# A hybrid decoder layer on one core: sample rows in four transfers beside x's parts, and the delta rule's state loads spread over its first steps

## The chip, the cores and the metric

The kernel runs on one core of a Trainium2 chip. Its time is the device time of one execution in microseconds (us); the lower the better. TensorE does the matrix products, VectorE and ScalarE the elementwise work, GpSimd small copies, memsets and some transfers, and SyncE (SP) issues most transfers.

## The reference, cut to what matters

One layer of a decoder trunk runs over 256 prompt tokens and over 8 sequences of 4 sample tokens, which go through the same weights:

```
proj = x @ w_in                                    # 2048 -> 11280 columns, split in 11 parts
y_a  = (gB * conv3(gC * h)) @ w_a_out              # short convolution mixer
q, k, v = silu(conv4([q | k | v]))                 # width-4 causal convolution
o, S = gated_delta_rule(l2norm(q), l2norm(k), v, g, beta, S0)   # 8 heads of 128, chunks of 64
y_b  = (rmsnorm(o) * silu(z)) @ w_b_out
merged = sigmoid(m_a) * y_a + sigmoid(m_b) * y_b
x = LN(ALPHA * x + merged @ w_o)
x = LN(ALPHA * x + relu(x @ w_up)**2 @ w_down)     # 2048 -> 8192 -> 2048
```

The prompt starts from zero states; the samples bring convolution states and a 128 x 128 state S0 for each head and sequence. All data are float32.

## The kernel before, in words

**The stream of weight blocks.** All products are one stream of blocks, numbered i. A block is 512 rows by 256 columns of a weight matrix, 512 KB, loaded by SP (`load`, L169). For precision each weight is split in two: ScalarE rounds it (`split_hi`, L177) and VectorE takes the rest (`split_lo`, through the helper `tt`, L140). The activations x are split likewise into `xh` and `xl`, with the 2048 features on 16 groups of 128 partitions and 288 columns (256 prompt, 32 sample tokens). `matmuls(i)` issues 24 matrix products for a block: for each of 4 groups of rows and 2 halves of columns the three products of L202, L203 and L204 (xh with hi, xl with hi, xh with lo). A list `fill` gives functions that are called one after each three products, so that other TensorE work stands between them. The first eight blocks belong to two column groups in turn, so that blocks 0 and 1 need features 0 to 511 only, blocks 2 and 3 the next, and so on.

**The order of the work.** It is written out by hand. In iteration i the program issues the high split of block i + 3, one step of a generator `sgen` (the delta rule's side work), one step of its helper `aux`, the low split of block i + 3, the work on finished sums (`due`), and then the products of block i. Engines take their instructions in this order, each its own; a waiting instruction holds up all that follow on its engine. High and low parts have four buffers each, so the split of block i + 3 waits for the products of block i - 1.

**The start.** x comes in four parts of 512 features (`xr0` to `xr3`), `xr0` in two halves, one issued by ScalarE (L728) and one by SP (L731). The sample tokens come in one transfer (L729) as 128 rows: quarter j of the features of token t is row 32 j + t, so that one row holds 512 features. TensorE turns blocks of 128 x 128 (transposes, L771 for the prompt, L757 for the samples); ScalarE casts the result to `xh` (L775, L760), VectorE takes `xl`. Eleven small products on a cleared tile (`warm_up`, L718) stand before, and four more between the samples' transposes and block 0. All of the samples' features are turned at once, after the prompt's first part; the prompt's other three parts are turned in the fills of blocks 1, 3 and 5. On GpSimd a one-element copy (L742) waits for the third part `xr2`; behind it stand 19 small loads of convolution states, convolution weights and norm weights (L745 to L751), which `hist_tiles` turns on TensorE before block 6 (L791 to L796).

**The delta rule.** Finished q, k and v columns go through `conv_evac`: a memset and a copy of the state on GpSimd (L261, L262), copies and a product on ScalarE (L263, L264, L266), three products on VectorE (L143), then SiLU on ScalarE (L276, L281), one block later. `sgen` first runs `gates` (from block 10, one step for each block), and then `gdn(G)` for the two halves of four heads, the first from block 20 on at the earliest. In `gdn`, four loads on GpSimd bring the states S0 (512 KB each, L911), three memsets clear `kqm`, `U128` and `aT` (L929, L931), and the first two steps turn k and q (L943) and take squares and copies (L945, L947); in the third step the sample's keys are spread by ScalarE into `wide` (L961), and in the fourth TensorE turns that (L965). `warm_up`, `x_sample` and `x_steps` are used only at the start.

## Time and profile before

| | before |
|---|---|
| median of 3 runs | 1711.37 us (1710.66 to 1711.64) |
| the profiled execution | 1709.66 us, of which its span 1707.8 |
| mean granted TensorE clock | 0.992 |
| TensorE busy | 1684.7 us (99%) |
| VectorE, ScalarE, GpSimd busy | 1012.4, 727.0, 123.5 us |
| read from memory | 270.19 MB, 163 GB/s over the span |

Busy times are shares of the whole span. With TensorE at 99%, the time can shrink only where TensorE waits or runs at a lower clock. The span counts from the first to the last instruction; some 1.9 us lie around it. A timeline row of the profile gives start, duration, engine, line, operation, output and inputs, how many, and in brackets how long the engine was idle before and what ended that. PE is TensorE, DVE VectorE, ACT ScalarE, POOL GpSimd.

### The profile page before, as it was taken

How to read it: one execution, taken by the hardware profiler on the slowest of the kernel's cores; microseconds unless marked ns; L12 is line 12 of the kernel's file. 1: busy time of each engine (PE TensorE's matmuls, PEld its weight loads, DVE VectorE, ACT ScalarE, POOL GpSimd, SP SyncE). 2: the span in 40 equal slices, each digit the busy share in tenths (PEclk: the TensorE clock that was granted, in tenths of full speed). 3: DMA queues.
4: the chain of work that ended last, by engine and by line, in shares of the span. 5: the costliest groups of instructions: out<-in, count | busy, mean ns of one | idle time of the engine just before them, and what ended most of it. 6: DMA issues, size and time to landing. Idle time of an engine off the chain costs nothing.

```text
span 1707.8 us, 31019 instructions
## 1 busy us (share of the span) xinstructions
PE 1684.7 (99%) x13040; PEld 1667.2 (98%) x13040; DVE 1012.4 (59%) x1292; ACT 727.0 (43%) x1045; POOL 123.5 (7%) x223
## 2 busy tenths in 40 slices
PE   8989999999999999999999999999999999999997
PEld 7989999999999999999999999999999999999996
DVE  4568795748544444456778844565445654466575
ACT  4675536433643334334445533344334433344331
POOL 2122331013300000000010000000000000000000
PEclk9999999999999999999999999999999999999998
DMA  8454356444655555555575555555555555555552
GB/s 242 149 173 150 112 172 208 146 135 137 186 177 164 170 161 169 164 165 165 158 198 176 169 166 165 167 163 166 168 161 160 171 163 170 163 162 160 173 160 69
DMA packets 272537, 279.69 MB, mean 164 GB/s; under 512 B 12109, under 2 KB 267533, under 8 KB 272265
## 3 DMA queue, kind: packets, MB, share of 16 engines
q1 hardware_dynamic: 267066, 265.26, 49.9%
q0 software_dynamic: 4352, 11.67, 2.5%
q8 instruction: 102, 1.67, 0.4%
q10 hardware_dynamic: 980, 0.79, 0.2%
q14 instruction: 37, 0.30, 0.0%
HBM read 270.19 MB, written 7.48 MB: 163 GB/s over the span
## 4 chain that ended last, share of the span: by engine, by line
PE 90%; DVE 2%; ACT 1%; issue 1%; POOL 0%; ACTq 0%; DVEq 0%
PE acc L202 29%; PE acc L203 29%; PE acc L204 29%; PE g L1069 1%; DVE lo L140 1%; DVE w L143 1%; PE g L1057 0%; PE g L1236 0%; PE g L1239 0%; PE g L1188 0%; PE g L1216 0%; PE g L598 0%; PE g L657 0%; DVE v L143 0%; ACT hi L177 0%
## 5 line engine op out<-in xcount | busy, mean ns | idle before, releaser
L140 DVE TENSOR_TENSOR lo<-raw,hi 128x1024 fp32r<-128x1024 f32 (+1 forms) x500 | 613.2, 1230 | 541.6 <-ACT hi L177 539.4
L177 ACT CAST hi<-raw 128x1024 fp32r<-128x1024 f32 (+1 forms) x500 | 518.1, 1039 | 756.5 <-PE acc L203 701.6
L202 PE MATMUL acc<-xh,hi 128*128 128x288 f32 x1408 | 421.4, 299 | 0.0
L204 PE MATMUL acc<-xh,lo 128*128 128x288 f32 x1408 | 416.4, 296 | 0.0
L203 PE MATMUL acc<-xl,hi 128*128 128x288 f32 x1408 | 416.4, 296 | 0.0
L202 PE MATMUL acc<-dh,hi 128*128 128x290 f32 x1024 | 303.9, 297 | 0.0
L203 PE MATMUL acc<-dl,hi 128*128 128x290 f32 x1024 | 303.3, 296 | 0.0
L204 PE MATMUL acc<-dh,lo 128*128 128x290 f32 x1024 | 302.7, 296 | 0.0
L204 PE MATMUL acc<-hh,lo 128*128 128x288 f32 x1024 | 302.3, 295 | 0.0
L203 PE MATMUL acc<-hl,hi 128*128 128x288 f32 x1024 | 302.3, 295 | 0.0
L202 PE MATMUL acc<-hh,hi 128*128 128x288 f32 x1024 | 302.2, 295 | 0.0
L202 PEld LDWEIGHTS acc<-xh,hi 128*128 128x128 f32 x1408 | 265.6, 189 | 2.0 <-issue 0.7
L203 PEld LDWEIGHTS acc<-xl,hi 128*128 128x128 f32 x1408 | 265.7, 189 | 1.0
L204 PEld LDWEIGHTS acc<-xh,lo 128*128 128x128 f32 x1408 | 265.5, 189 | 0.0
L202 PEld LDWEIGHTS acc<-dh,hi 128*128 128x128 f32 x1024 | 193.6, 189 | 0.1
L204 PEld LDWEIGHTS acc<-dh,lo 128*128 128x128 f32 x1024 | 193.3, 189 | 0.0
L203 PEld LDWEIGHTS acc<-dl,hi 128*128 128x128 f32 x1024 | 193.3, 189 | 0.1
L203 PEld LDWEIGHTS acc<-hl,hi 128*128 128x128 f32 x1024 | 192.4, 188 | 0.0
L204 PEld LDWEIGHTS acc<-hh,lo 128*128 128x128 f32 x1024 | 192.3, 188 | 0.0
L202 PEld LDWEIGHTS acc<-hh,hi 128*128 128x128 f32 x1024 | 192.1, 188 | 0.0
L203 PE MATMUL acc<-ml,hi 128*128 128x288 f32 x256 | 75.6, 295 | 0.0
L204 PE MATMUL acc<-mh,lo 128*128 128x288 f32 x256 | 75.6, 295 | 0.0
(394 smaller groups left out, 1602.8 us busy)
## 6 DMA issues: line engine op xcount, KB each, us to landing
raw<-in_w_in_dram SPq DMA_DIRECT2D x176, 512.0 KB, 3.5
raw<-in_w_up_dram SPq DMA_DIRECT2D x128, 512.0 KB, 3.8
raw<-in_w_down_dram SPq DMA_DIRECT2D x128, 512.0 KB, 3.6
raw<-in_w_o_dram SPq DMA_DIRECT2D x32, 512.0 KB, 3.7
raw<-in_w_a_out_dram SPq DMA_DIRECT2D x16, 512.0 KB, 3.6
raw<-in_w_b_out_dram SPq DMA_DIRECT2D x16, 512.0 KB, 3.6
S<-in_state_gdn_dram POOLq DMA_DIRECT2D x8, 512.0 KB, 7.8
out_dram<-S POOLq DMA_DIRECT2D x8, 512.0 KB, 4.5
```

The source lines that it names most:

```text
L140: dve.tensor_tensor(out=out, in0=a, in1=b, op=op)
L143: dve.scalar_tensor_tensor(out=out, in0=a, scalar=s, in1=b, op0=o0, op1=o1)
L177: act.copy(his[i][:, k:k + step], raw[i][:, k:k + step])
L202: pe.matmul(o, wh, xh_, start=st, stop=False)
L203: pe.matmul(o, wh, xl_, start=False, stop=False)
L204: pe.matmul(o, wl, xh_, start=False, stop=en)
L1069: pe.matmul(out[r, q * 64:q * 64 + 64], a[r, q, :], b[r, q, :], start=True, stop=True)
```

## The change

The sample rows are now (token, quarter): row 4 t + j, column p of transfer c is feature 512 c + 128 j + p of token t. There are four transfers of 64 KB on ScalarE's queue, one for each part of x; the first stands ahead of ScalarE's half of `xr0`. So one transpose for each part gives four groups of features. The first part's stands between the transposes of the two halves of `xr0`, and the other three stand in the fills of blocks 1, 3 and 5, beside the prompt's transposes. The first weight block comes in two transfers of 256 KB. Nine warm-up products stand at the start instead of eleven, and two before block 0 instead of four. Block 0's splits are issued one group of rows at a time, and the cast of the second half of `xr0` stands behind the first two of them. In the delta rule, the four loads of states and the memsets of `aT` and `U128` are issued in successive steps, and `sgen` starts at block 8 instead of 10.

```
-    warm_up(11)
+    warm_up(9)
...
-    xsr = A["x_sample"].rearrange("b t (j f) -> j (b t) f", j=4)
+    xsr = A["x_sample"].rearrange("b t (c j p) -> c (b t) j p", j=4, p=P)
...
+    act.dma_start(xs4[:, 0:P], xsr[0])
     act.dma_start(xr[0][:, :, 256:512], xpr[:, :, 256:512])
-    act.dma_start(xs4, xsr)
+    for c in range(1, 4):
+        act.dma_start(xs4[:, c * P:c * P + P], xsr[c])
     sp.dma_start(cf[:, 0:128], A["cf"][:, 0:128])
     sp.dma_start(xr[0][:, :, 0:256], xpr[:, :, 0:256])
-    load(0)
+    load(0, 2)
...
-    def x_sample():
+    def x_sample(i):
         g = gtile()
-        for c in range(4):
-            pe.transpose(g[:, c * P:(c + 1) * P], xs4[:, c * P:(c + 1) * P], ident)
-        gv = g.rearrange("p (c j t) -> p j c t", c=4, j=4)
-        xv, xw = (u.rearrange("p (j c) t -> p j c t", j=4)[:, :, :, NP_:NT] for u in (xh, xl))
+        pe.transpose(g[:, 0:P], xs4[:, i * P:(i + 1) * P], ident)
+        gv = g[:, 0:P].rearrange("p (t j) -> p j t", j=4)
+        xv, xw = (u[:, 4 * i:4 * i + 4, NP_:NT] for u in (xh, xl))
         act.copy(xv, gv)
         tt(xw, gv, xv, SUB)
...
         S0 = pl.tile([P, 4, 8, P], F32, tag="S0", name=nm("S0"))
-        for hh in range(4):
+
+        def states_in(hh):
             gps.dma_start(S0[:, hh], A["state_gdn"][0, :, 4 * G + hh].rearrange("b d e -> d b e"))
...
         gps.memset(kqm, 0.0)
-        for z in (U128, aT):
-            gps.memset(z, 0.0)
+        states_in(0)
...
         act.copy(wide, four(kst))
+        states_in(1)
         yield
...
+        states_in(2)
         yield
...
         tt(glx[:, 1], glf, glx[:, 0], SUB)
-        yield
-        yield
+        states_in(3)
+        yield
+        gps.memset(aT, 0.0)
+        yield
+        gps.memset(U128, 0.0)
...
-    for f in x_steps(0):
-        f()
-    x_sample()
-    warm_up(4)
-    split_hi(0, 1)
-    split_lo(0, 1)
+    (t0, o0), (t1, o1) = (f() for f in x_steps(0))
+    for g in t0:
+        g()
+    o0()
+    x_sample(0)
+    for g in t1:
+        g()
+    warm_up(2)
...
+    for k in range(KB):
+        act.copy(his[0][:, k], t[:, k])
+        tt(los[0][:, k], t[:, k], his[0][:, k], SUB)
+        if k == 1:
+            o1()
...
         if i in (1, 3, 5):
-            a_, b_ = x_steps(i // 2 + 1)
+            a_, s_, b_ = x_fill(i // 2 + 1)
             idle = lambda: None
-            fill.extend([idle, idle, idle, a_, idle, b_])
+            fill.extend([idle, idle, a_, s_, idle, b_])
...
-        if i > 9 and sgen:
+        if i > 7 and sgen:
```

More of the change, by code (lines that the diff above doesn't have):

```diff
@@ L161, in at, with load @@
         due.setdefault(i, []).append(f)
-    def load(i):
+    def load(i, step=KB):
         if i >= len(blocks):
@@ L168, in load @@
         t = wp.tile([P, KB, GW], F32, tag="raw", name=nm("raw"))
-        sp.dma_start(t, gi["W"][r0:r0 + KB * P, gi["col0"]:gi["col0"] + GW]
-                     .rearrange("(k p) c -> p k c", p=P))
+        src = gi["W"][r0:r0 + KB * P, gi["col0"]:gi["col0"] + GW].rearrange("(k p) c -> p k c", p=P)
+        for k in range(0, KB, step):
+            sp.dma_start(t[:, k:k + step], src[:, k:k + step])
         raw[i] = t
@@ L766, in prompt @@
             gv = g.rearrange("p (k t) -> p k t", k=2)
-            steps = []
             def turn(k, b):
@@ L777, in prompt, with x_fill, step @@
             return [turn(k, b) for k in range(2) for b in range(2)], out
-        def step(part):
+        return lambda: prompt(0), lambda: prompt(1)
+    def x_fill(i):
+        def step(u):
             def f():
-                turns, out = part()
+                turns, out = x_steps(i)[u]()
                 for g in turns:
@@ L785, in step @@
             return f
-        return [step(lambda: prompt(0)), step(lambda: prompt(1))]
+        return step(0), lambda: x_sample(i), step(1)
     def hist_tiles():
@@ L1321, in hybrid_kernel @@
     aux = []
-    for f in x_steps(0):
-        f()
-    x_sample()
-    warm_up(4)
-    split_hi(0, 1)
-    split_lo(0, 1)
+    (t0, o0), (t1, o1) = (f() for f in x_steps(0))
[6 more added lines that the diff above has]
+    warm_up(2)
+    his[0] = wp.tile([P, KB, GW], F32R, tag="hi", name=nm("hi"))
+    los[0] = wp.tile([P, KB, GW], F32R, tag="lo", name=nm("lo"))
+    t = raw.pop(0)
+    for k in range(KB):
[3 more added lines that the diff above has]
+            o1()
     rest = [lambda: sp.dma_start(cf[:, 128:], A["cf"][:, 128:NE]),
```

## The prediction

> **What bounds the kernel.** TensorE is busy for 99% of the span, so I read only what holds it up: the waits of TensorE, then the timelines around the two long ones.

> ```profile
> PE g L965 <- ACT vmh L961: 6.0, 1, 6.0
> PE g L757 <- DMA xs<-in_x_sample_dram: 3.8, 1, 3.8
> PE g L644 <- DVE R L140: 2.6, 1, 2.6
> ```

> The third lies in the tail, which is not edited. The second is the start (timeline):

> ```profile
> 5.86 1.63 PE L771 MATMUL g<-cf,xr 128*128 128x128 f32 x8
> 11.26 1.11 PE L757 MATMUL g<-cf,xs 128*128 128x128 f32 x4 [3.77 <-DMA xs<-in_x_sample_dram]
> 12.89 2.36 ACT L177 CAST hi<-raw 128x256 fp32r<-128x256 f32 x6
> 13.52 0.80 PE L202 MATMUL acc<-xh,hi 128*128 128x288 f32 x1
> 14.12 0.44 PE L203 MATMUL acc<-xl,hi 128*128 128x288 f32 x1
> ```

> The prompt's first part is turned by 7.5; all else waits for the sample rows, issued at 1.25 and landed at 11.26. ScalarE splits no weight until they are cast. The DMA view of 4:10.5 shows the rows' queue (q10) trickling, 129 packets while q1 moves 1315:

> ```profile
> q1 hardware_dynamic: 1315, 1.49, 91.5%
> q10 hardware_dynamic: 129, 0.26, 14.4%
> ```

> After the idle time TensorE runs at half clock (windows of 12:17: PEclk 0.50): matmuls follow each other every 0.24 us until 17.3, then every 0.133.

> The first wait is GpSimd's queue, then ScalarE's, then TensorE's (timelines):

> ```profile
> 95.09 3.59 POOL L911 DMA_DIRECT2D S<-in_state_gdn_dram  x4
> 98.67 1.08 POOL L929 MEMSET b<- 128x1152 f32 x1
> ...
> 101.50 0.22 POOL L262 COPY w<-hw 128x24 f32<-128x24 f32 x1
> ```

> ```profile
> 101.76 0.56 ACT L266 ACTIVATE w<-w,hw 128x312 f32<-128x312 f32 x1 [2.37 <-POOL w L262]
> 105.63 1.28 ACT L276 ACT_TABLE_LOAD   x1
> 109.35 0.62 ACT L961 COPY vmh<-kqs 128x512 f32<-128x512 f32 x1
> ```

> ```profile
> 110.02 1.12 PE L965 MATMUL g<-cf,vmh 128*128 128x128 f32 x4 [6.01 <-ACT vmh L961]
> 110.79 0.59 PE L202 MATMUL acc<-xh,hi 128*128 128x288 f32 x1
> 111.18 0.44 PE L203 MATMUL acc<-xl,hi 128*128 128x288 f32 x1
> ```

> Loads and memsets, 6.5 us on GpSimd, stand ahead of the two tiny pieces that the convolution needs (L261, L262); ScalarE waits in order, so the copy `wide` (L961) is late.

> **The start, term by term.** Nine warm-up matmuls of 0.43 from 1.19 end at 5.0. The x half that came last landed at 5.7 (issue 1.18, 4.5 to landing), the other at 4.2; now 64 KB of sample rows go ahead of one, and no rows trickle beside them. `cf`, also 64 KB in 512-byte rows, landed in 2.5. I take 5.2 (4.2 to 6.7). ScalarE's first cast begins 1.1 later, as before (6.96 against 5.86): 6.3 to 6.9. The quarter's cast (0.2 to 0.4, rows L264 and L263) and the first cast of weights, 0.4, follow: 7.4, if the half weight block has landed. Up to it 1.1 MB must move (`cf` 64 KB, samples 256, x 512, half a block 256); from 0.5 MB at 4.0 (windows: 29, 215 and 254 GB/s in 1:4) at 268 GB/s (DMA view) that is 6.3. VectorE: 0.69 for the part, 0.25 for the quarter, 0.42 for the first low part: 8.1. From there 22 matmuls remain of block 0, at full clock 2.9: block 1 begins at 11.0, against 18.60 before. Weight splits keep ahead: VectorE has the block's last low part at 9.9. Gain 7.6.

> Moved out: three sample transposes now stand in the fills of blocks 1, 3 and 5; two such (L958, L959) cost 0.21 between matmuls, so 0.3 in all. Their casts and subtractions, 0.2 and 0.25, hide under blocks of 3.19. `out` of the second x half goes behind two weight casts; TensorE wants it 12 matmuls later.

> What is late next is the history (L791 to L796). Its 19 loads on GpSimd start when the third x part lands (18.6); the last is issued at 31.80 and needs 3.2, so it is there at 35.0, and TensorE asks at 37.97. It will ask at 30.7, so that x part must land by 14.3. Up to it 4.0 MB move (four weight blocks 2048 KB, three x parts 1536, samples 256, `cf` 64): at the 360 GB/s of the DMA view 11:14, when nothing trickled, by 13.7; at 300, by 15.7. I charge 0.3 (0 to 4.3, the latter if it lands no earlier). **Start: 7.6 − 0.3 − 0.3 = 7.0.**

> Queues: ScalarE issues five transfers instead of two (0.5 to 1.1 each), and the last waits for the first quarter's landing, as they share a counter; behind it stands the table load (1.28). That ends by about 5.3, hidden, as the first cast is at 6.3. On SP the third weight piece now waits for `cf`, x part 1 for x half 0, later ones for a quarter; what is already issued keeps SP's queue moving to beyond 8 us, so I charge nothing.

> **The delta rule.** The chain before, from ScalarE's timeline, for the three blocks before L965: weight casts 3 × 0.95, the first stage (L945, L947) 2 × 2.48, two convolution pieces 2 × 0.95, the small copies 0.62, `wide` 0.62: 11.0. Added to it were waits for GpSimd of 1.89 and 2.37, a table load of 1.28 and four SiLUs of 1.0: 17.5. TensorE needs 3 × 3.19 for the blocks, 2 × 0.88 and 0.2 for transposes: 11.5. The difference, 6.0, is the wait shown.

> After: the gates start at block 8, not 10, and the rule at 20, not 21, so the gates' GpSimd copies (2.55) end two blocks earlier. Per step only one load (0.9) and one memset (1.1), later one of either, stand before a convolution's piece, and GpSimd reaches them ahead of ScalarE. On the old time axis: gate results at 84.0, copies to 86.5, memset and load to 88.5, the piece 88.7; ScalarE wants it at 92.9. `wide` now precedes the SiLUs, whose table is already loaded. So all four additions go, 11.0 against 11.5, if ScalarE starts block 20 on time. Its gate work does not run over: block 15 begins at 71.5 and takes 5.7, blocks 16 and 17 1.9 each (to 81.0); block 18, from 81.1, takes 0.95, 2.6 for exponentials and 2.3 for table and SiLUs (87.0); block 19 0.95 (88.0); block 20 starts at 88.9. Gain: block 24 began at 110.79 and would at 100.58 + 3.19 + 0.44 = 104.2, so 6.6; then it took 4.21 instead of 3.19 at half clock, 1.0 more. **7.6.** A margin of 0.5 may be wrong by a convolution's wait (2.4), so 5.2 to 7.6. The remaining memsets and the second rule's loads are wanted blocks later; there TensorE never waited for them. Shifting the rule by one block moves the other small waits (L1161 0.3, L1236 0.2) by at most 0.5 either way.

> **Sum.** 7.0 + 7.6 = 14.6. The profiled execution took 1709.66 (span 1707.8): 1695.1. The runs' median is 1711.37, 1.7 above it: **1696.8**.

> [...]

> **Rivals.**
> 1. *The x part that releases the history is no earlier* (18.6): the wait of 4.3 at L791 to L796 replaces 0.3; gain 10.6: 1700.8. For: q1 moved 1.49 MB in 6.5 us, a pace at which its 3.6 MB last to near 18. Against: 360 GB/s in 11:14. Chance 0.14.
> 2. *Half clock at the start.* Four warm-ups fewer, and a hole of 0.2 to 0.7 at 5.0: block 0's 22 matmuls at 0.24 cost 2.4 more: 1699.2. For: the clock was still half at 13 to 17 with TensorE at work, and the first warm-ups step by 0.43 like the last four at PEclk 0.50, though the page gives them 1.00. Against: PEclk is 1.00 after them and falls (0.74) only in 10:11, after three idle us. 0.13. [...]
> 3. *ScalarE is still late at L961*, by one GpSimd wait: 2 to 2.4 stay: 1699.0; were all of it to stay, 1704.4. 0.12.
> 4. *The quarters trickle too*, so the change does not spread them: 64 KB at q10's 0.04 MB/us is 1.6 more before x half 0 lands: 1698.4. 0.03.
> 5. *Slower*: the first quarter lands late and ScalarE's queue stands behind its fifth transfer. It is hidden up to a landing at 4.5 (4.5 + 0.5 + 1.28 = 6.3); each us beyond costs one; the gain is used up at 19.1, and from 22.5 on it is slower by over 0.2%: at 25, 1717. For: the whole transfer took 10.0; against: `cf` took 2.5. 0.02.

> **Numbers.** The forecast has 0.56, own range 1695 to 1698.5. Downward, the bounds of small terms (history 0.3, x half 0.2, small waits 0.5) and the spread of the runs (1710.66 to 1711.64, so 1.0) give 1694.8; upward, rivals 1 to 4 reach 1700.8, and two of them together 1702. So 1694.8 to 1702.0, with some 0.15 left out. What a measurement can tell from no change is about 0.2%, 3.4 us: the forecast and rivals 1 to 4 gain more (0.96, when 0.02 is kept for several at once, which counts as same); slower is rival 5, 0.02.

> **Right or wrong.** Right: first matmul of L203 near 7.4 and block 1 near 11; PEclk 1.0 from about 7 on; no wait of TensorE for `xs`; no wait at L970 (old L965) for the copy; no table load between convolution and copy. Wrong: a wait of TensorE for `hwr` or `lnr` (rival 1), PEclk 0.5 within 7 to 12 (rival 2), a wait for `vmh` over 1 us (rival 3), or a first ScalarE cast beyond 8 us (rivals 4, 5).

## The result and the profile after

| | before | after |
|---|---|---|
| median, the two side by side | 1711.01 us (4 runs, 1709.46 to 1711.64) | 1697.90 us (4 runs, 1697.17 to 1700.09) |
| the profiled execution, its span | 1709.66, 1707.8 us | 1700.09, 1698.3 us |
| TensorE busy, mean granted clock | 1684.7 us, 0.992 | 1681.4 us, 0.994 |

The ratio is 0.9927, 95% interval [0.991, 0.9944]: 13.1 us faster. The forecast was 1696.8 us with a range from 1694.8 to 1702.0, so the time lies inside it. The sum behind it holds only in part, and the profile shows where. The lines of the changed kernel that are named here stand one to nine lower than those of before.

The waits of TensorE in the changed kernel (total us, times, longest us; the tail's 2.6 for `R` is as before and not shown):

```profile
PE g L800 <- DMA lnr<-in_gdn_norm_w_dram: 1.3, 1, 1.3
PE g L772 <- DMA xr<-in_x_prompt_dram: 1.3, 2, 0.7
...
PE acc L204 <- DVE xl L140: 1.0, 1, 1.0
PE g L799 <- DMA har<-in_conv_a_w_dram: 0.9, 1, 0.9
```

The waits of 6.0 for `vmh` and 3.8 for `xs` are gone. In their place stand `lnr` and `har`, which are history tiles, `xr`, which is the second half of x part 0 and then x part 1, and `xl`, the low part of x part 1, which block 2 needs.

The start, from TensorE's timeline:

```profile
5.29 0.27 PE L759 MATMUL g<-cf,xs 128*128 128x128 f32 x1
6.30 0.66 PE L772 MATMUL g<-cf,xr 128*128 128x128 f32 x4 [0.74 <-DMA xr<-in_x_prompt_dram]
...
7.04 0.48 PE L203 MATMUL acc<-xh,hi 128*128 128x288 f32 x1
...
10.49 0.29 PE L203 MATMUL acc<-xh,hi 128*128 128x288 f32 x1
```

The first product stands at 7.04 and block 1 at 10.49. Then the history. Before, on GpSimd and on TensorE:

```profile
18.63 0.18 POOL L742 COPY hwr<-xr 1x1 f32<-1x1 f32 x1 [17.72 <-DMA xr<-in_x_prompt_dram]
...
31.80 0.49 POOL L751 DMA_DIRECT2D lnr<-in_gdn_norm_w_dram  x1 [1.41 <-DMA har<-in_state_conv_a_dram]
```

```profile
37.97 0.25 PE L796 MATMUL g<-cf,lnr 33*128 33x33 f32 x1
```

And in the changed kernel:

```profile
16.88 0.18 POOL L745 COPY hwr<-xr 1x1 f32<-1x1 f32 x1 [15.97 <-DMA xr<-in_x_prompt_dram]
...
30.17 0.49 POOL L754 DMA_DIRECT2D lnr<-in_gdn_norm_w_dram  x1
```

```profile
33.41 0.26 PE L799 MATMUL g<-cf,har 76*128 76x76 f32 x1 [0.94 <-DMA har<-in_conv_a_w_dram]
...
35.17 0.28 PE L800 MATMUL g<-cf,lnr 33*128 33x33 f32 x1 [1.33 <-DMA lnr<-in_gdn_norm_w_dram]
```

And what the idle time brings with it: the windows of 36:40 (busy us of PE, PEld, DVE, ACT, POOL with their instruction counts; then PEclk, DMA share, GB/s):

```profile
36.00:38.00 2.00, 2.00 (x10) 2.00 (x10) 0.29 (x1) 0.12 (x2) 0.36 (x1) 0.50 1.07 307
38.00:40.00 2.00, 2.00 (x10) 2.00 (x10) 0.00 (x0) 0.00 (x0) 0.00 (x0) 0.50 0.68 187
```

TensorE is busy throughout, but at half clock. The delta rule, by contrast, runs as forecast: `wide` (L965 now) comes 9.7 us earlier than before, and TensorE goes on without a wait.

```profile
99.62 0.62 ACT L965 COPY vmh<-kqs 128x512 f32<-128x512 f32 x1
...
100.64 0.60 PE L970 MATMUL g<-cf,vmh 128*128 128x128 f32 x4
```

Since every kernel here issues the products of the weight blocks in the same order, the start of the first product of a block can be set against that of before. This **lead** (before minus run, us, one profiled execution each) is the measure in what follows. The two changes of the diff, start and delta rule, separate in it at block 8: up to there the start works, and from there on the side work of the delta rule.

| kernel | block 1 | 2 | 4 | 6 | 8 | 32 | last | median us |
|---|---|---|---|---|---|---|---|---|
| changed kernel | 8.11 | 6.92 | 5.42 | 2.76 | 0.00 | 7.55 | 9.34 | 1697.90 |
| e1_delta_only | 1.48 | 1.49 | 1.50 | -0.09 | -0.08 | 7.47 | 9.30 | 1700.18 |
| e2_start_only | 8.06 | 7.79 | 6.91 | 3.00 | 1.67 | 0.77 | 0.77 | 1708.09 |
| e3_history_early | 7.59 | 6.36 | 4.86 | 4.75 | 4.76 | 12.32 | 14.12 | 1695.86 |
| e4_one_transfer | 5.52 | 5.52 | 5.52 | 3.82 | 3.82 | 2.36 | 2.36 | 1707.06 |
| e5_spread_gates10 | 7.59 | 7.48 | 6.21 | 3.39 | 3.40 | 5.45 | 5.45 | 1703.98 |
| e6_gates8_bunched | 7.55 | 7.27 | 6.44 | 2.99 | 1.70 | 8.44 | 10.25 | 1698.58 |
| e7_rows_whole | 5.65 | 5.64 | 5.64 | 5.64 | 5.65 | 13.17 | 14.97 | 1693.68 |
| e8_quarters_late | 8.03 | 6.72 | 6.54 | 6.42 | 6.43 | 13.98 | 15.78 | 1693.81 |
| e9_cover_wait | 7.64 | 7.38 | 6.43 | 3.23 | 3.23 | 10.75 | 12.57 | 1696.54 |
| e10_rows_gpsimd | 7.06 | 6.16 | 4.67 | 4.57 | 4.58 | 12.13 | 13.95 | 1695.41 |
| after_again | 7.57 | 7.38 | 5.88 | 3.10 | 0.36 | 7.87 | 9.69 | 1697.56 |

Read the first row: 8.1 us of lead at block 1, nothing of it left at block 8, 9.3 at the end. In this profiled execution the whole edit of the start is worth nothing. It is the worst of its kind: e2, e5, e6 and after_again have the same start, and keep 1.67, 3.40, 1.70 and 0.36 at block 8. The lead at block 1 is uncertain too: e1 has the start of before and still leads there by 1.48, mostly because TensorE ran at half clock for 3.4 us there and not for 6.8. The kernel before had medians of 1710.06, 1710.44 and 1709.87 us beside the three groups e1 to e4, e5 to e8, and e9, e10 and after_again.

### The profile page after: what moved, and what is told of

Its sections match the earlier page's. It is cut to its first block, busy times and chain, and to the rows that moved or that the text cites. A ratio compares the mean times of both kernels' runs of the same rounds, so it can differ in the third digit from the quotient of the medians.

```text
span 1698.3 us, 31025 instructions
## 1 busy us (share of the span) xinstructions
PE 1681.4 (99%) x13036; PEld 1665.4 (98%) x13036; DVE 1011.8 (60%) x1295; ACT 726.7 (43%) x1048; POOL 132.6 (8%) x223
## 3 DMA queue, kind: packets, MB, share of 16 engines
q8 instruction: 102, 1.67, 0.4%
HBM read 270.19 MB, written 7.48 MB: 164 GB/s over the span
## 4 chain that ended last, share of the span: by engine, by line
PE 97%; DMA 2%; DVE 0%; issue 0%; SPq 0%; POOL 0%; ACTq 0%; ACT 0%
PE acc L203 31%; PE acc L205 31%; PE acc L204 31%; DMA xr<-in_x_prompt_dram 1%; PE g L1078 1%; DMA hwr<-in_state_gdn_conv_dram 1%; PE g L1066 0%; PE g L1225 0%; PE g L1245 0%; PE g L1248 0%; DMA lnr<-in_gdn_norm_w_dram 0%; PE g L820 0%; PE g L1197 0%; PE g L1237 0%; PE g L599 0%; PE g L947 0%
## 5 line engine op out<-in xcount | busy, mean ns | idle before, releaser
L140 DVE TENSOR_TENSOR lo<-raw,hi 128x1024 fp32r<-128x1024 f32 (+1 forms) x500 | 614.5, 1232 | 550.6 <-ACT hi L178 548.4
L203 PE MATMUL acc<-xh,hi 128*128 128x288 f32 x1408 | 421.9, 300 | 0.0
L203 PE MATMUL acc<-dh,hi 128*128 128x290 f32 x1024 | 303.9, 297 | 0.0
L203 PE MATMUL acc<-hh,hi 128*128 128x288 f32 x1024 | 302.2, 295 | 0.0
L203 PEld LDWEIGHTS acc<-xh,hi 128*128 128x128 f32 x1408 | 265.6, 189 | 2.0 <-issue 0.7
L203 PEld LDWEIGHTS acc<-dh,hi 128*128 128x128 f32 x1024 | 193.6, 189 | 0.1
L203 PEld LDWEIGHTS acc<-hh,hi 128*128 128x128 f32 x1024 | 192.1, 188 | 0.0
```

The costliest lines, as they stand in the source:

```text
L140: dve.tensor_tensor(out=out, in0=a, in1=b, op=op)
L203: pe.matmul(o, wh, xh_, start=st, stop=False)
```

## The experiments

**e1_delta_only** and **e2_start_only** split the change. e1 is the kernel before with only the delta rule's lines of the diff (the four `states_in` and the memsets of `aT` and `U128` in successive steps), and

```
-        if i > 9 and sgen:
+        if i > 7 and sgen:
```

and e2 is the changed kernel with these lines as before.

> The start of the kernel before, with the delta rule's part of the change (loads and memsets spread, side work from block 8). Theory A (the delta part alone made the profiled gain, as the block starts of the changed kernel say: the lead of 8.1 us at block 1 is down to 0.0 at block 8, and grows to 7.5 at block 25 and 9.3 at block 114): 8 to 9.5 us faster than before, 1701.5 to 1703, with no wait of TensorE for vmh at the turned keys. Theory B (both parts give what the prediction charged, 7.0 and 7.6, and the profiled execution was an unlucky one): 7.6 faster, 1703.5, so A and B differ only in e2.

> The start of the changed kernel with the delta rule of the kernel before. Theory A (what the start gains is given back before block 6, where the history's transposes wait for loads that the third x part releases, and at half clock after that wait): at most 3 us faster than before, 1708 to 1711, with a lead of about 8 at block 1 and of 0 to 3 at block 8, and waits of TensorE for har and lnr. Theory B (the start is worth 7.0): 1704, lead at block 8 still near 7.

e1: 1700.18 us, ratio 0.9942 [0.9927, 0.9957]; e2: 1708.09 us, 0.9987 [0.9977, 0.9996]. The delta rule brings 9.9 us, a little more than the 8 to 9.5 expected, and the start 2.0, in the medians. The start has its 8.06 at block 1, 6.91 at block 4, and loses 5.2 of that up to block 8, where TensorE waits for the history:

```profile
PE g L800 <- DMA lnr<-in_gdn_norm_w_dram: 2.1, 1, 2.1
...
PE g L799 <- DMA har<-in_conv_a_w_dram: 0.7, 1, 0.7
```

**e3_history_early**: the release of the history alone.

```
-    gps.tensor_copy(hwr[0:1, 0:1], xr[2][0:1, 0, 0:1])
+    gps.tensor_copy(hwr[0:1, 0:1], xr[0][0:1, 0, 0:1])
```

> The changed kernel, but the one-element copy on GpSimd that holds back the 19 history loads waits for the first x part instead of the third. Theory A (the loads' release is what eats the gain): no wait at the history's transposes, no half clock in 30 to 40 us, lead at block 8 about 5, time 1691.5 to 1694. Rival (the transfers of the first 30 us are all that the DMA engines can carry, so that history loads at 6 us push x parts 1 to 3 and weight blocks 2 and 3 back by as much): lead at block 6 under 3, waits for xr or raw instead, time 1696 to 1699.

1695.86 us, ratio 0.9916 [0.9901, 0.993]. On GpSimd and TensorE:

```profile
4.69 0.18 POOL L745 COPY hwr<-xr 1x1 f32<-1x1 f32 x1 [3.79 <-DMA xr<-in_x_prompt_dram]
...
18.34 0.48 POOL L754 DMA_DIRECT2D lnr<-in_gdn_norm_w_dram  x1
```

```profile
33.21 0.25 PE L800 MATMUL g<-cf,lnr 33*128 33x33 f32 x1
```

The last load is issued 11.8 us earlier, no wait stands in brackets, and the lead of block 4 (4.86) is still there at block 8 (4.76). So the loss between blocks 4 and 8 is the history's; 0.1 us of it remains. The lead at block 8 is the one that theory A expected (about 5), and yet the time missed its 1691.5 to 1694 us. The 5 us are what the profiled execution of the changed kernel lost. By the medians less was lost: the start keeps 2.0 us (e2), and the earlier release brings 2.0 more (1697.90 to 1695.86), not 5.

A second loss comes before block 4: the lead falls from 7.59 to 4.86 here and from 8.11 to 5.42 in the changed kernel. There it is weight block 2 that is late (ScalarE of the changed kernel, the bracket tells how long it sat idle):

```profile
13.99 1.05 ACT L178 CAST hi<-raw 128x1024 fp32r<-128x1024 f32 x1 [3.39 <-DMA raw<-in_w_in_dram]
```

**e4_one_transfer**: the kernel before, its one sample transfer kept, only the row order turned to (token, quarter).

```
-    xsr = A["x_sample"].rearrange("b t (j f) -> j (b t) f", j=4)
+    xsr = A["x_sample"].rearrange("b t (j f) -> (b t) j f", j=4)
...
-        gv = g.rearrange("p (c j t) -> p j c t", c=4, j=4)
+        gv = g.rearrange("p (c t j) -> p j c t", c=4, j=4)
```

> The kernel before, with the sample rows still in one transfer of 256 KB, but ordered (token, quarter) so that the outermost dimension on the memory side is 32 instead of 4. Theory C (the rows trickled because an outermost 4 puts them on few DMA engines, not because the transfer is large): it lands near 5 to 7 us instead of 11.3, first matmul of block 0 near 8 to 9, lead at block 1 some 5 us, of which the history leaves little: 1707 to 1711. Rival (one large transfer beside x is slow as such, and four small ones are needed): still lands past 10, time 1710 to 1712.

1707.06 us, ratio 0.9982 [0.9973, 0.9992]. The same 256 KB in rows of the same length land 5.1 us after their issue instead of 10.0 (issue view of 0:14), and their transposes wait for nothing:

```profile
xs<-in_x_sample_dram ACTq DMA_DIRECT2D x1, 256.0 KB, 5.1
```

```profile
7.41 0.60 PE L757 MATMUL g<-cf,xs 128*128 128x128 f32 x4
```

All transfers together moved 350 GB/s in 4:10 instead of 267. So the trickle was the order of the rows, not the size of the transfer, and about two thirds of the lead at block 1 (5.5 of 8.1) come without any split. Of the 5.5, 1.1 are the clock: block 0 took 4.0 us in e4, at full clock, and 5.1 before, in part at half. The old order has the 4 quarters outermost on the memory side, the new one the 32 tokens. No view here shows engine by engine, but the trace records the start and duration of each packet. Of the 128 packets of 2 KB that carry the rows, never more than four were under way at once before (but for 0.03 us), and up to 15 in e4. So the landing, the lead and the time are as theory C expected, and the packets fit it; which engines took them is not shown.

**e5_spread_gates10** and **e6_gates8_bunched** split the delta rule's edit. e5 is the changed kernel with

```
-        if i > 7 and sgen:
+        if i > 9 and sgen:
```

and e6 keeps the start at block 8 but issues the four loads and three memsets together, as before.

> The changed kernel with the side work starting at block 10 again, as before; the loads and memsets stay spread. Theory A (the spread alone takes the memsets out of the way of the wide turn, and the start of the side work at block 8 only moves it): TensorE's 6.0 us wait for vmh is gone and the gain in the delta rule stays at 7 to 8 us, so 1697.5 to 1699.5 us, within 1.5 us of the changed kernel. Rival B (it is the earlier start that makes the room): the wait stays at 4 us or more and the time is 1703 to 1706 us.

> The changed kernel with the state loads and memsets in one place again, as before; the side work still starts at block 8. Theory A (the bunch is the cause): the wait for vmh of about 6 us is back, about 7 us of gain are lost, 1704 to 1706 us. Rival B (two blocks of earlier side work are enough to hide GpSimd's 10 us): no such wait, 1697 to 1699 us.

e5: 1703.98 us, ratio 0.9964 [0.9951, 0.9977]; e6: 1698.58 us, 0.9928 [0.9911, 0.9944]. From block 8 to block 32 e5 gains 2.05 and e6 6.74, where both edits together gain 7.55. These gains carry an uncertainty of 1 to 1.5: e2 and e4, whose delta rule is that of before, lose 0.90 and 1.46 in the same stretch. The waits of TensorE, first of e5, then of e6:

```profile
PE g L970 <- ACT vmh L965: 3.8, 1, 3.8
```

```profile
PE g L969 <- ACT vmh L965: 0.6, 1, 0.6
```

Rival B holds in essence, by both times (its wait of 4 us or more in e5 is 3.8): the side work's earlier start carries the gain. In e6 the bunch still stands ahead of a convolution's pieces, and ScalarE still waits for it, but for 1.16 us only, and 6.5 us ahead of the copy (GpSimd and ScalarE):

```profile
85.77 3.60 POOL L915 DMA_DIRECT2D S<-in_state_gdn_dram  x4
...
92.56 0.56 ACT L267 ACTIVATE w<-w,hw 128x312 f32<-128x312 f32 x1 [1.16 <-POOL w L263]
...
99.01 0.62 ACT L965 COPY vmh<-kqs 128x512 f32<-128x512 f32 x1
```

In e5 the wait of 1.89 for the gates' copies and the table load ahead of `wide` are back, and only the 2.37 behind the bunch is gone: 6.0 becomes 3.8. The spread alone is worth what that one wait was. Beside the earlier start it is worth nothing that the medians show: the ratio of e6 is 0.9928, that of the changed kernel 0.9927.

**e7_rows_whole**, **e8_quarters_late** and **e10_rows_gpsimd** ask where the loss before block 4 comes from. In the traces of before and of the changed kernel the transfers of SP and ScalarE share eight completion counters in turn, and a transfer waits for the landing of the one that had its counter before (the ninth of the changed kernel, on SP at 2.76 us, for `cf`); with the quarters and the half weight block ahead of it, x part 1 is issued at 6.27 us instead of 2.75; SP waited 2.8 us for it, until ScalarE's half of x part 0 had landed (6.26). All three are e3_history_early with the sample rows issued in another way (e7 also turns them with four transposes ahead of block 0):

```
-    act.dma_start(xs4[:, 0:P], xsr[0])             # e7 alone
+    act.dma_start(xs4, xsr)                        # e7: one transfer, in the order of e4
...
-    for c in range(1, 4):
-        act.dma_start(xs4[:, c * P:c * P + P], xsr[c])
...
     load(2)
+    sp.dma_start(xs4[:, P:2 * P], xsr[1])          # e8
     load(3)
     sp.dma_start(xr[2], xpr[:, :, 1024:1536])
+    for c in range(2, 4):
+        sp.dma_start(xs4[:, c * P:c * P + P], xsr[c])   # e8
...
+    for c in range(1, 4):
+        gps.dma_start(xs4[:, c * P:c * P + P], xsr[c])  # e10: first on GpSimd's queue
```

> The changed kernel with the history released by x part 0 (as in e3_history_early) and the sample rows in one transfer in the order (token, quarter), issued first, all four transposes ahead of block 0. Three transfers fewer are in flight. Theory C (in the changed kernel x part 1 and weight block 2 are issued late, at 6.3 and 6.7 us, because each transfer waits for the landing of the one eight before it): x part 1 is issued before 4 us and weight block 2 before 5 us, the loss of 2.6 us in blocks 1 to 3 is gone, block 0 starts up to 1 us later; 1693.5 to 1695.5 us (e3_history_early 1695.9). Rival D (the transfers run at the full rate anyway and only their order matters): the same loss, or block 0 at 9 us as in e4_one_transfer, 1696 to 1698 us.

> As e3_history_early, with the last three quarters of the sample rows issued by SyncE behind x part 1, weight block 2 and x part 2, so that five transfers fewer stand ahead of x part 1. Theory C (late issue by the wait for the transfer eight before): x part 1 is issued at about 3.5 us and weight block 2 at about 5 us, block 0 keeps its start near 7.1 us, and the loss in blocks 1 to 3 falls from 2.6 us to under 1 us: 1693 to 1694.5 us. Rival D (rate-bound): no gain over 1695.9 us, weight block 2 lands no earlier than in e3_history_early.

> As e3_history_early, with the last three quarters of the sample rows issued by GpSimd ahead of everything else on its queue. Theory C (in e3_history_early x part 1 and weight block 2 are held up by the wait for the transfer eight before; in e8_quarters_late quarter 1 came 1.0 us too late instead): x part 1 is issued near 3.3 us, no wait for xs, the loss between blocks 1 and 4 is 0.5 to 1 us, 1692.5 to 1693.7 us. Rival D (weight block 2 is bound by the rate of all transfers): the same cast of weight block 2 near 13 us as in e8_quarters_late and a loss of 1.5 us or more, 1693.8 to 1695 us.

e7: 1693.68 us, ratio 0.9903 [0.9888, 0.9918]; e8: 1693.81 us, 0.9902 [0.9887, 0.9917]; e10: 1695.41 us, 0.9914 [0.9901, 0.9928]. By time theory C seems right for e7 and e8, but its mechanism is not. e8's SP and ScalarE:

```profile
3.25 0.51 SPq L735 DMA_DIRECT2D xr<-in_x_prompt_dram  x1
3.91 0.41 SPq L171 DMA_DIRECT2D raw<-in_w_in_dram  x1
```

```profile
12.88 1.04 ACT L178 CAST hi<-raw 128x1024 fp32r<-128x1024 f32 x1 [2.87 <-DMA raw<-in_w_in_dram]
```

Weight block 2 is issued 2.8 us earlier than in the changed kernel (3.91 against 6.69) and arrives 1.1 us earlier (12.88 against 13.99). In e10 it is again issued near 4 us (4.00) and arrives at 14.74, later than in e3 (14.55); its time lies above both ranges, and neither theory has all its signs: C's loss of 0.5 to 1 us is 2.4, and D's cast near 13 is not there. And e2, with the start of the changed kernel, issues it at 6.23 and has it at 12.53, before e8. So the time of issue does not set the landing; that it is the other transfers under way is argued, not shown. Between e3 and e7 the sample rows are the same bytes: ScalarE's queue (q10) needs 848 packets for them and the half x part in e3, 16.2% of the engines' time in 2:14, and 411 packets, 13.6%, in e7. Which of the other transfers holds weight block 2 back in each case stays open. e7 gives up 2.5 us at block 1 (its block 0 starts at 9.22, 2 us later and not up to 1 as expected) and loses nothing after it; e8 starts as early as the changed kernel and loses 1.5, of which 1.0 is a wait for quarter 1. Both beat the changed kernel by 4 us, 2 of which are the earlier history of e3, and they stand side by side, so in none of the three placings tried do four transfers have an advantage over one in the right order.

**e9_cover_wait** and **after_again** ask what the half clock costs. e9 is the changed kernel with

```
         if i == 6:
+            cover = gtile()
+            for _ in range(14):
+                pe.matmul(cover, warm[:, 0:P], warm, start=True, stop=True)
             hist_tiles()
```

> The changed kernel with 14 products of the cleared tile (some 0.21 us each at full clock, 3 us) ahead of the history's transposes, so that TensorE works while it would wait for the history. Their result is used nowhere. Theory A (of the 5.3 us that the changed kernel loses between blocks 5 and 8, half is the wait and half the half clock that the idle time brings): the history is turned at the same time, blocks 6 and 7 take 3.2 us each instead of 5.9 and 3.3 to 4, PEclk stays at 1.00 from 34 to 42 us, and the time falls by 2 to 2.6 us against the changed kernel: 1695 to 1696.3 us. Rival B (the clock falls for another reason, such as the small transposes): PEclk still 0.5 at 36 to 40 us, no gain or 0.5 us lost, 1697.5 to 1699 us.

> The changed kernel once more, beside e10_rows_gpsimd on one chip: 1697 to 1698.5 us. If the whole lead of the start is lost at the history in every execution, block 8 starts again at 44.6 us; if it depends on when the last history load lands, between 42.5 and 45 us.

e9: 1696.54 us, ratio 0.9921 [0.9906, 0.9936]; after_again: 1697.56 us, 0.9929 [0.9917, 0.9942], with block 8 at 44.26. In e9 block 6 still starts late, but the lead stays 3.23 from there to block 8, and the windows show full clock; the same stretch of after_again shows half:

```profile
37.00:39.00 2.00, 2.00 (x18) 2.00 (x17) 0.00 (x0) 0.73 (x1) 0.00 (x0) 1.00 0.88 268
```

```profile
37.00:39.00 2.00, 2.00 (x10) 2.00 (x9) 0.00 (x0) 0.00 (x0) 0.00 (x0) 0.50 0.78 180
```

So theory A holds for the two profiled executions: of the loss of after_again 2.8 us are the wait (lead 5.88 to 3.10) and 2.7 the clock (3.10 to 0.36), and e9, with work in the idle time, loses the first alone. The pair does not show by itself that the work saved the clock, since e5 kept the full clock through the same wait without it; the last section returns to this. The profiled execution is 3.0 us shorter (span 1697.9 to 1694.9). In the medians e9 gains only 1.0 and just misses the expected 1696.3. The runs of after_again suggest why: the profiled one has 1699.7 us at a mean granted clock of 0.994, the other four 1696.84 to 1698.49 us at 0.995 to 0.996. If most executions lose less to the clock than the profiled one, e9 can give back only what they lose.

## Why the prediction was right, and where it was not

**The start, 7.0 forecast.** The term of 7.6 at block 1 was nearly right: 7.04 for the first product (forecast 7.4) and 10.49 for block 1 (forecast 11.0), a lead of 8.1. The last half of x part 0 landed at 6.26 instead of the 5.2 taken, but that cost little: ScalarE's first cast needed the other half alone (5.49), and the first product waited for the half weight block, which was there at 6.55 (forecast 6.3). After that two terms failed.

- *History, 0.3 charged, bounds 0 to 4.3.* This is the step that failed. The third x part landed at 16.88 instead of the 14.3 that the step needed. Its rate was right: from 4 us on 336 GB/s, between the 300 and 360 taken. Its amount was not: the step let 4.0 MB move up to that landing, as if transfers ended in the order of their issue, and 4.82 MB had moved by then (DMA view of 0:16.83), so 0.8 MB of transfers issued later, from 9.17 on, had moved beside it. The chain behind the copy was right up to the last issue, 13.3 us (before 13.2), but the last load then needed 4.9 us to land instead of 3.2. So it came at 35.1, as before (35.0), while TensorE reached the history 5.3 us earlier (31.84, before 37.16).

  The price was 2.7 of waiting and 2.7 of half clock in the profiled execution, 5.4 in all, beyond the upper bound, which had no term for the clock. The prediction's own sign of rival 1 (0.14) came with it, a wait for `lnr`; but rival 1 as written had the x part land no earlier than 18.6, and it landed 1.7 earlier. Its price, too, had no term for the clock. That TensorE ran at half clock after the idle time before block 0 (PEclk 0.50 in 12:17) stood in the prediction's own first section; it was applied to the waits that the change removes and not to the wait that it might bring.
- *Weight splits "keep ahead", x part 1 "charge nothing".* Between blocks 1 and 4 the lead falls by 2.7 in the profiled execution (1.7 in after_again, 1.15 in e2), where 0.2 was forecast for the transposes. Weight block 2 arrives at 13.99 (in e2, with the same start, at 12.53), and ScalarE sat idle for 3.39 before it.

What is left at block 8 is 0.0 to 3.4 us in the five profiled executions with this start, and 2.0 in the medians (e2), not 7.0.

**The delta rule, 7.6 forecast.** From block 8 to block 32 it gained 7.55, and e1 alone 7.55. The chain was right: no wait at L970, no table load between convolution and copy, `wide` at 99.62. Its cause was put down too broadly to both edits. The earlier start alone brings 6.74 and the spread alone 2.05, so the spread is worth 0.8 once the start is earlier, which is within the uncertainty of these gains. Beyond the forecast another 1.8 us came between blocks 32 and 112. In that stretch TensorE is busy 317.44 of 318.38 us before and 316.60 of 316.60 after: 0.9 of idle time and 0.8 of busy time less. The prediction gave this shift of the side work "0.5 either way". e6 has the same 1.8 and e5 none, so it too comes with the earlier start.

**The sum.** 14.6 was forecast. The profiled execution gained 9.6 (1709.66 to 1700.09), the medians 13.1. By terms, the start's 2.0 (e2) and the delta rule's 9.9 (e1) make 11.9, which is near the 12.3 between the medians beside after_again: 5 us too much stood on the start and over 2 too little on the delta rule. The two errors cancel in part. That the number was right is in part luck, and half of its explanation was wrong.

**The rivals.** Half clock in block 0 (0.13) did not come: PEclk was 1.00 from 4 to 32 us, and 0.50 only behind the history's wait. ScalarE late at L961 (0.12) did not come, and e5 shows what it would have been: a wait of 3.8. That the quarters trickle (0.03) and the slower case (0.02) did not come. One transfer in place of the four deserved more thought: the 10.0 us of the sample rows were an effect of their order, as e4 shows (5.1), and with the order mended one transfer of 256 KB (e7) does 2.2 us better than four of 64 KB (e3), and as well as the best placing of four (e8).

## What to carry to other kernels

When a stage at the front is made faster, find the next input that it will ask for and follow that input's own chain back to its first release; a chain with a fixed length (here 13 us of small loads behind one copy) takes most or all of the gain unless its release moves too, and the idle time can cost as much again in clock (here 2.7 us beside 2.7 of waiting). Before splitting a slow transfer, look at the order of its dimensions: here the outermost dimension alone was worth 5 of 10 us. Where one edit has two halves, run each half: an earlier start of the side work did what the careful spreading was credited with.

## What the runs showed of the hardware

The clock does not follow from the length of the wait alone. Almost the same wait for `lnr`, 2.4 us in e5 and 2.5 in after_again, left it whole in e5 and halved it for 6.8 us in after_again; in e2 and e6 the half clock lasted 3.4 us. In each of the thirteen traces, the times between changes of the granted clock, up to the last fall at the end of the kernel, are whole multiples of 3.41 us (3.41, 6.83, 10.24, 27.31, 30.72 and so on), so each trace can be cut into stretches of 3.41 us, counted from its changes. Cut so, after_again looks like this around the wait, and e5 like the second pair (the second number is TensorE's busy time):

```profile
30.94:34.35 3.41, 1.43 (x13) 1.14 (x11) 2.70 (x3) 3.41 (x5) 0.00 (x0) 1.00 0.85 175
34.35:37.77 3.42, 2.95 (x12) 2.91 (x13) 1.48 (x2) 0.90 (x4) 0.73 (x2) 0.50 0.81 213
```

```profile
30.12:33.53 3.41, 2.01 (x17) 1.64 (x15) 2.29 (x4) 3.07 (x4) 0.25 (x1) 1.00 1.03 230
33.53:36.95 3.42, 2.35 (x17) 2.34 (x18) 1.99 (x2) 1.41 (x5) 0.70 (x2) 1.00 0.71 208
```
